# Down projections of a two-layer decoder trunk: both halves of the activation in one 512-column matmul

## The chip, the core and the metric

The kernel runs on one core of one Trainium2 chip. Five engines work side by side and meet through semaphores: TensorE (PE; its weight loads are shown as PEld), VectorE (DVE), ScalarE (ACT), GpSimd (POOL) and SyncE (SP), which issues the large DMAs. TensorE writes its sums to PSUM, eight banks of 512 float32 columns on 128 partitions; everything else lies in SBUF. The metric is the device time of one execution in microseconds (us). The kernel before takes 921.43 us, the median of three runs (919.47 to 921.58).

## The reference

The reference is a two-layer decoder trunk over 256 tokens of width 1024, in float32. Each layer has a mixer (layer 0: softmax attention beside Mamba-2 heads; layer 1: gated DeltaNet), then a gated feed-forward network, then a gated embedding of the layer. The change is inside the feed-forward network, which both layers have:

```python
D_MODEL = 1024
SEQ = 256
D_FF = 2816

def conv_ffn(h, w_gate, w_up, conv_w, conv_b, w_down):
    gte = causal_dwconv(h @ w_gate, conv_w) + conv_b.astype(h.dtype)
    return (jax.nn.silu(gte) * (h @ w_up)) @ w_down

...
        h = rmsnorm(x, norm_ffn[i])
        x = x + conv_ffn(h, ffn_w_gate[i], ffn_w_up[i], ffn_conv_w[i], ffn_conv_b[i], ffn_w_down[i])
        x = x + per_layer_embedding(x, p[i], norm_ple[i], ple_w_proj[i], ple_w_gate[i])
```

The down projection is the last product, `... @ w_down`: 2816 input features to 1024 output features for 256 tokens.

## The kernel before, in words

Activations lie transposed: features on the 128 partitions, the 256 tokens along the free dimension (`T = 256`). A matrix of 1024 features is eight tiles of 128x256, one of 2816 features is 22 tiles (`NF`).

TensorE takes float32r operands in one pass, with less precision than float32. To keep the precision, the kernel splits each operand in a high half and a low half, and `mm3` adds three products per tile of 128 input features: high weight by high activation (L188), high weight by low activation (L189), low weight by high activation (L190). Each is a matmul with 128x128 weights and 256 moving columns, and each has its own weight load, so the high weights are loaded twice.

Weights arrive in pieces of up to 1024 columns. `piece` (L140) issues the DMA from the packed stream on SP, ScalarE rounds it to the high half `whi` (L163), and VectorE, in some places GpSimd, takes the rest as the low half `wlo` (L164). Raw pieces and both halves have four buffers each, and the two split instructions are issued at a raised priority (`AHEAD = 80`), so they stand in their engines' queues well before the matmuls that use them. The order on each engine is set by the tile scheduler from those priorities; there is no table of orders. The name `lead` in `piece` shifts where a piece starts inside its buffer; it is used at two of the 22 steps of the gate and up projections alone.

Activations that TensorE streams come from `moving` (L105): one tile in which halves lie one behind the other, 256 columns each, and which starts 48 elements after an aligned address. High half and low half of one feature tile are neighbours there.

`ffn` (L277) runs in three steps. First, 22 times, gate and up tiles are made, convolved, gated and split into `ys`. Then, for each of the eight output tiles `m`, 22 feature tiles are added up in a PSUM bank `pd`, in three pieces of 8, 7 and 7 feature tiles (L310 to L314). VectorE multiplies the sum by the norm factor `Rf` on the way out (L316), adds it to the residual `x[m]` (L317), and `norm_tile` starts the next norm: ScalarE and VectorE split `x[m]` times a gain to `xp`, ScalarE squares it to `nsq`, GpSimd adds the squares up to `nss`. Last, `ple_proj` projects the layer's embedding (`pp`, 48 matmuls), `norm_end` sums the squares over partitions (`nps`, one-column matmuls at L255 and L256) and computes the norm factor, and `ple` makes the gate (`pgt`). The seven PSUM banks of the tag `acc` go round among `pg`, `pu`, `pd`, `pp` and `pgt`. So there are two stretches of down projection, one in each layer, with 8 x 22 x 3 = 528 matmuls each.

Elsewhere in the kernel, the value projection of layer 0 (L607 to L609) already has matmuls with 512 moving columns: there the weights move and the activation stands.

Of the kernel before, what the change touches and what calls it, by code (L numbers as in the profile page):

```python
# [11 lines left out]
AF = mybir.ActivationFunctionType  # L12
ALU = mybir.AluOpType
# [9 lines left out]
T = 256  # L23
# [28 lines left out]
class Trunk:  # L52
    def __init__(self, ctx, tc, stream, xT, pT, pv, tok, cst, out):
        self.tc, self.nc, self.ctx = tc, tc.nc, ctx
        self.stream, self.out = stream, out
        self.off = 0
        self.order = []
        self.n = 0
        self.pshare, self.share = 0.0, 0.0
        nc = self.nc  # L60
        ep = ctx.enter_context
        self.cpool = ep(tc.tile_pool(name="cpool", bufs=1))
        self.rawp = ep(tc.tile_pool(name="rawp", bufs=4))
        self.splp = ep(tc.tile_pool(name="splp", bufs=4))
        self.smallp = ep(tc.tile_pool(name="smallp", bufs=3))
        self.chain = ""
        self.nrm = ep(tc.tile_pool(name="nrm", bufs=1, space=PSUM))

        self.xx = self.moving(self.cpool, 2 * KD, "xx")
        warm = self.cpool.tile([P, 1], F32, tag="warm", name="warm")  # L70
        nc.vector.memset(warm, 0.0)
        nc.scalar.activation(warm, warm, AF.Exp)

        zt = self.cpool.tile([P, 256], F16, tag="zt", name="zt")
        nc.vector.memset(zt, 0.0)
        pz = self.nrm.tile([P, 512], F32, tag="nrm", name="pwarm")
        for _ in range(WARM):
            nc.tensor.matmul(pz[:, :T], zt[:, :P], zt, start=True, stop=True)
        self.pv = self.cpool.tile([P, NPV], F32, tag="pv", name="pv")
        nc.scalar.dma_start(self.pv, pv)  # L80
        xs = self.cpool.tile([P, KD, T], F32, tag="x", name="x")
        for m in range(0, KD, 2):
            nc.sync.dma_start(xs[:, m:m + 2], xT[:, m:m + 2])
        self.x = [xs[:, m] for m in range(KD)]
        self.tok = self.cpool.tile([P, 64], F32, tag="tok", name="tok")
        self.cst = self.cpool.tile([P, NCC], F32, tag="cst", name="cst")
        self.cst_src, self.tok_src = cst, tok
        self.pT = pT
        self.ones = self.cpool.tile([P, 1], F32, tag="ones", name="ones")
        nc.gpsimd.memset(self.ones, 1.0)  # L90
        self.ident = self.c("ident")
        self.id16 = self.cpool.tile([P, P], F16, tag="id16", name="id16")
        self.zb = [[self.cpool.tile([P, 4, P], F16, tag=f"zb{s}_{l}", name=f"zb{s}_{l}") for l in range(6)]
                   for s in range(1)]
# [10 lines left out]
    def moving(self, pool, n, tag):  # L105

        t = pool.tile([P, 48 + n * T], F32R, tag=tag, name=self.uid(tag), bufs=1, align_bytes=256)
        return [t[:, 48 + i * T:48 + (i + 1) * T] for i in range(n)]

    def uid(self, s):  # L110
        self.n += 1
# [69 lines left out]
    def mm3(self, out, w, a, start=True, stop=True):  # L181

        nc = self.nc
        n = len(a)
        for k in range(n):
            wh, wl = w[0][:, k], w[1][:, k]
            ah, al = a[k]
            nc.tensor.matmul(out, wh, ah, start=start and k == 0, stop=False)  # L188
            nc.tensor.matmul(out, wh, al, start=False, stop=False)  # L189
            nc.tensor.matmul(out, wl, ah, start=False, stop=stop and k == n - 1)  # L190

    def rsqrt(self, src, n, dst=None):
        nc = self.nc
        s = self.small(n, "ri", I32)
        y = self.small(n, "ry")
        nc.vector.tensor_scalar(out=s, in0=src.bitcast(I32), scalar1=1, scalar2=None,
                                op0=ALU.logical_shift_right)
        nc.vector.tensor_scalar(out=y.bitcast(I32), in0=s, scalar1=-1, scalar2=0x5F3759DF,
                                op0=ALU.mult, op1=ALU.add)
        for it in range(3):  # L200
            t = self.small(n, "rt")
            t2 = self.small(n, "rt")
            o = dst if (it == 2 and dst is not None) else self.small(n, "ry")
            nc.vector.scalar_tensor_tensor(out=t, in0=y, scalar=-0.5, in1=y, op0=ALU.mult, op1=ALU.mult)
            nc.vector.tensor_tensor(t2, t, src, op=ALU.mult)
            nc.vector.scalar_tensor_tensor(out=o, in0=t2, scalar=1.5, in1=y, op0=ALU.add, op1=ALU.mult)
            y = o
        return y
# [68 lines left out]
    def ffn(self, i, nxt):  # L277
        nc, tc = self.nc, self.tc
        with self.psum(acc=7), tc.tile_pool(name=f"ffn{i}", bufs=3) as fp:
            ys = []  # L280
            yy = self.moving(fp, 2 * NF, "yy")
            for f in range(NF):
                pg, pu = self.acc("pg"), self.acc("pu")
                both = ((pg, "ffn_w_gate"), (pu, "ffn_w_up"))

                ws = self.piece([(n, i, 0, KD, f * P, P) for _, n in both],
                                lead={KICK: (0, 16), KICK + 1: (32, 48)}.get(f, (0, 0)))
                for (ps, _), w in zip(both, ws):
                    self.mm3(ps[:, :T], w, self.a)
                g = fp.tile([P, T], F32, tag="g", name=self.uid("g"))  # L290
                nc.vector.tensor_tensor(g, pg[:, :T], self.R, op=ALU.mult)
                cw = lambda t: self.v(f"fcw{i}", f * 3 + t)
                h = fp.tile([P, T], F32, tag="h", name=self.uid("h"))
                nc.scalar.activation(h, g, AF.Identity, scale=cw(2), bias=self.v(f"fcb{i}", f))
                for s in (1, 2):
                    nc.vector.scalar_tensor_tensor(out=h[:, s:], in0=g[:, :T - s], scalar=cw(2 - s), in1=h[:, s:],
                                                   op0=ALU.mult, op1=ALU.add)
                sl = fp.tile([P, T], F32, tag="sl", name=self.uid("sl"))
                si = nc.scalar.activation(sl, h, AF.Silu)
                if i == 0 and f < len(self.zb[0]):  # L300
                    with tc.issue_after(si.ins):
                        nc.scalar.activation(self.zb[0][f], self.ident.unsqueeze(1).to_broadcast([P, 4, P]), AF.Copy)
                y = fp.tile([P, T], F32, tag="y", name=self.uid("y"))
                nc.vector.tensor_tensor(y, sl, pu[:, :T], op=ALU.mult)
                yh, yl = yy[2 * f:2 * f + 2]
                self.split(y, yh, yl)
                ys.append((yh, yl))
            self.norm_begin(f"ple{i}", fp)
            Rf = self.R
            for m in range(KD):  # L310
                pd = self.acc("pd")
                for k0, nk in ((0, 8), (8, 7), (15, 7)):
                    wd, = self.piece([("ffn_w_down", i, k0, nk, m * P, P)])
                    self.mm3(pd[:, :T], wd, ys[k0:k0 + nk], start=k0 == 0, stop=k0 == 15)  # L314
                d = fp.tile([P, T], F32, tag="pleg", name=self.uid("d"), bufs=4)
                nc.vector.tensor_tensor(d, pd[:, :T], Rf, op=ALU.mult)  # L316
                nc.vector.tensor_tensor(self.x[m], self.x[m], d, op=ALU.add)  # L317
                self.norm_tile(m)
            self.ple_proj(i, fp)
            self.norm_end()  # L320
            self.ple(i, nxt, fp)
# [831 lines left out]
```

## Time and profile before

| what | value |
|---|---|
| runs | 919.47, 921.43, 921.58 us |
| the profiled execution's own time | 923.28 us |
| its span, first to last instruction | 921.5 us |
| TensorE clock granted, mean over the span | 0.992 of full |
| PE busy | 98% of the span, 7834 matmuls |
| PEld busy | 93%, 7834 weight loads |
| DVE busy | 81% |
| ACT busy | 63% |
| down projection, layer 0 | 313.44 to 373.28 us |
| down projection, layer 1 | 827.20 to 887.04 us |

The profile is of one execution. A matmul's duration in it (276 ns for 256 columns) is longer than its share of TensorE's time, because matmuls are pipelined: the next begins before the one ahead has ended. What one costs is read from the distance between two starts. TensorE has two clock levels, 1.2 and 2.4 GHz; the granted clock is shown as 0.50 or 1.00.

### The profile page before, as it was taken

Reading aid. Unit: us, or ns where it says so; the run is one execution under the profiler, and the core shown is the slowest. Engines: PE = TensorE matmul, PEld = TensorE weight load, DVE = VectorE, ACT = ScalarE, POOL = GpSimd, SP = SyncE. Lnnn points to the kernel's source line nnn. Section 1 sums busy time; section 2 is a strip of 40 time slices with the busy share of each in tenths; the row PEclk is TensorE's granted clock in tenths of the full one; section 3 lists DMA queues with packets and bytes.
Section 4 is the critical chain, followed back from the end, with each engine's and each line's share of the span. In section 5 each row is a group of like instructions: output and inputs, shape, how many; then the busy total and the mean of one; then the engine's idle time right before and its main releaser. Section 6 shows DMA issues by size and latency. Waiting matters only on the chain. (4 is left out here: it accounts for less than half of the span.)

```text
span 921.5 us, 19977 instructions
## 1 busy us (share of the span) xinstructions
PE 900.1 (98%) x7834; PEld 860.1 (93%) x7834; DVE 747.3 (81%) x1662; ACT 584.8 (63%) x1237; POOL 42.9 (5%) x53
## 2 busy tenths in 40 slices
PE   8999999999999999999989999999999999999997
PEld 6988778999999999989889999999999999999997
DVE  6977778988888767789979998999868888876665
ACT  6577555667565545667678778787755665554552
POOL 0000112110000001010000000000002000000100
PEclk9999999999999999999989999999999999999999
DMA  7534332466666566545413333432345666666571
GB/s 276 181 122 131 93 114 92 140 197 193 203 186 197 177 203 209 169 138 158 141 47 93 114 100 108 119 113 88 122 134 177 184 194 199 190 193 189 179 227 48
DMA packets 40990, 141.40 MB, mean 153 GB/s; under 512 B 4672, under 2 KB 6208, under 8 KB 40896
## 3 DMA queue, kind: packets, MB, share of 16 engines
q1 hardware_dynamic: 40608, 139.84, 48.6%
q8 instruction: 61, 1.00, 0.4%
q10 hardware_dynamic: 288, 0.29, 0.1%
q14 instruction: 33, 0.27, 0.1%
HBM read 139.06 MB, written 1.05 MB: 152 GB/s over the span
## 5 line engine op out<-in xcount | busy, mean ns | idle before, releaser
L163 ACT ACTIVATE whi<-raw 128x1024 fp32r<-128x1024 f32 (+2 forms) x266 | 277.7, 1044 | 176.8 <-PE pd L189 38.6
L164 DVE TENSOR_TENSOR wlo<-raw,whi 128x1024 fp32r<-128x1024 f32 (+2 forms) x266 | 319.8, 1202 | 81.8 <-ACT whi L163 79.7
L188 PE MATMUL pg<-xx,whi 128*128 128x256 f32 x352 | 97.4, 277 | 0.6 <-DVE x L703 0.3
L188 PE MATMUL pu<-xx,whi 128*128 128x256 f32 x352 | 97.5, 277 | 0.0
L189 PE MATMUL pg<-xx,whi 128*128 128x256 f32 x352 | 97.4, 277 | 0.0
L189 PE MATMUL pu<-xx,whi 128*128 128x256 f32 x352 | 97.4, 277 | 0.0
L190 PE MATMUL pu<-xx,wlo 128*128 128x256 f32 x352 | 97.4, 277 | 0.0
L190 PE MATMUL pg<-xx,wlo 128*128 128x256 f32 x352 | 97.2, 276 | 0.0
L188 PE MATMUL pd<-yy,whi 128*128 128x256 f32 x352 | 97.2, 276 | 0.0
L189 PE MATMUL pd<-yy,whi 128*128 128x256 f32 x352 | 97.2, 276 | 0.0
L190 PE MATMUL pd<-yy,wlo 128*128 128x256 f32 x352 | 97.2, 276 | 0.0
L188 PE MATMUL pgd<-xx,whi 128*128 128x256 f32 x256 | 76.1, 297 | 0.4 <-DVE z L989 0.4
L190 PE MATMUL pgd<-xx,wlo 128*128 128x256 f32 x256 | 75.0, 293 | 0.0
L189 PE MATMUL pgd<-xx,whi 128*128 128x256 f32 x256 | 74.8, 292 | 0.0
L188 PEld LDWEIGHTS pg<-xx,whi 128*128 128x128 f32 x352 | 66.1, 188 | 0.8 <-issue 0.8
L188 PEld LDWEIGHTS pu<-xx,whi 128*128 128x128 f32 x352 | 66.1, 188 | 0.0
L189 PEld LDWEIGHTS pu<-xx,whi 128*128 128x128 f32 x352 | 66.1, 188 | 0.0
L190 PEld LDWEIGHTS pu<-xx,wlo 128*128 128x128 f32 x352 | 66.1, 188 | 0.0
L189 PEld LDWEIGHTS pg<-xx,whi 128*128 128x128 f32 x352 | 66.1, 188 | 0.0
L190 PEld LDWEIGHTS pg<-xx,wlo 128*128 128x128 f32 x352 | 66.1, 188 | 0.0
L188 PEld LDWEIGHTS pd<-yy,whi 128*128 128x128 f32 x352 | 66.1, 188 | 0.0
L189 PEld LDWEIGHTS pd<-yy,whi 128*128 128x128 f32 x352 | 66.1, 188 | 0.0
(357 smaller groups left out, 2636.1 us busy)
## 6 DMA issues: line engine op xcount, KB each, us to landing
raw<-stream SPq DMA_DIRECT2D x232, 512.0 KB, 3.6
raw<-stream SPq DMA_DIRECT2D x32, 448.0 KB, 3.3
x<-xT SPq DMA_DIRECT2D x4, 256.0 KB, 4.9
out<-x SPq DMA_DIRECT2D x8, 128.0 KB, 1.9
cst<-cst SPq DMA_DIRECT2D x1, 645.0 KB, 7.1
raw<-pT SPq DMA_DIRECT2D x2, 256.0 KB, 2.5
pv<-pv ACTq DMA_DIRECT2D x1, 215.5 KB, 4.4
raw<-stream SPq DMA_DIRECT2D x1, 128.0 KB, 2.0
```

Of the source, the lines that this page charges most:

```text
L163: nc.scalar.activation(hi, raw[:, :cols], AF.Copy)
L164: self.lo_engine(lo).tensor_tensor(lo_, raw[:, :cols], hi.bitcast(F32), op=ALU.subtract)
L188: nc.tensor.matmul(out, wh, ah, start=start and k == 0, stop=False)
L189: nc.tensor.matmul(out, wh, al, start=False, stop=False)
L190: nc.tensor.matmul(out, wl, ah, start=False, stop=stop and k == n - 1)
```

## The change

`moving` now also keeps, for each high half, a slice of 512 columns that covers the high half and the low half behind it. A new function `mm2` replaces `mm3` in the down projections: the high weights multiply both halves in one matmul of 512 columns, which fills the whole bank `pd`, and the low weights multiply the high half with 256 columns, added to the second half of the bank. The bank then holds high by high in its first 256 columns, and the two small products in its second. On the way out ScalarE copies the second half to SBUF, VectorE adds the first half to it, multiplies by `Rf`, and adds to the residual.

```diff
         t = pool.tile([P, 48 + n * T], F32R, tag=tag, name=self.uid(tag), bufs=1, align_bytes=256)
-        return [t[:, 48 + i * T:48 + (i + 1) * T] for i in range(n)]
+        ps = [t[:, 48 + i * T:48 + (i + 1) * T] for i in range(n)]
+        self.keep += ps
+        for i in range(0, n, 2):
+            self.both[id(ps[i])] = t[:, 48 + i * T:48 + (i + 2) * T]
+        return ps
...
+    def mm2(self, ps, w, a, start=True, stop=True):
+
+        nc = self.nc
+        n = len(a)
+        for k in range(n):
+            wh, wl = w[0][:, k], w[1][:, k]
+            ah, al = a[k]
+            nc.tensor.matmul(ps, wh, self.both[id(ah)], start=start and k == 0, stop=False)
+            nc.tensor.matmul(ps[:, T:], wl, ah, start=False, stop=stop and k == n - 1)
...
-                    self.mm3(pd[:, :T], wd, ys[k0:k0 + nk], start=k0 == 0, stop=k0 == 15)
+                    self.mm2(pd, wd, ys[k0:k0 + nk], start=k0 == 0, stop=k0 == 15)
                 d = fp.tile([P, T], F32, tag="pleg", name=self.uid("d"), bufs=4)
-                nc.vector.tensor_tensor(d, pd[:, :T], Rf, op=ALU.mult)
+                nc.scalar.activation(d, pd[:, T:], AF.Copy)
+                nc.vector.tensor_tensor(d, d, pd[:, :T], op=ALU.add)
+                nc.vector.tensor_tensor(d, d, Rf, op=ALU.mult)
                 nc.vector.tensor_tensor(self.x[m], self.x[m], d, op=ALU.add)
```

On TensorE only the down projections differ; every other matmul keeps its place in the queue. These are TensorE's rows around the first matmul of layer 0's down projection before, from the end of the up projection (`pu`) on:

```order
L190 MATMUL pu_4130<-xx_70,wlo_4140 128x256
L188 MATMUL pu_4130<-xx_70,whi_4139 128x256
L189 MATMUL pu_4130<-xx_70,whi_4139 128x256
L190 MATMUL pu_4130<-xx_70,wlo_4140 128x256
L188 MATMUL pd_4204<-yy_2568,whi_4207 128x256
L189 MATMUL pd_4204<-yy_2568,whi_4207 128x256
L190 MATMUL pd_4204<-yy_2568,wlo_4208 128x256
```

And now:

```order
L195 MATMUL pu_4130<-xx_70,wlo_4140 128x256
L193 MATMUL pu_4130<-xx_70,whi_4139 128x256
L194 MATMUL pu_4130<-xx_70,whi_4139 128x256
L195 MATMUL pu_4130<-xx_70,wlo_4140 128x256
L204 MATMUL pd_4204<-yy_2568,whi_4207 128x512
L205 MATMUL pd_4204<-yy_2568,wlo_4208 128x256
```

Three matmuls of 256 columns have become one of 512 and one of 256; over both layers that is 1056 matmuls before and 704 now, with the same number of columns.

On ScalarE the scheduler also moves the last tile's steps. ScalarE's rows at the end of the down projection in layer 0 before, where the `whi` of 5085 is the second piece of the gate after it, `nsq_4948` the square of the last residual tile and `pp` the copies of the embedding's projection:

```order
L163 ACTIVATE whi_5079<-raw_5077 128x1024
L163 ACTIVATE whi_5085<-raw_5083 128x1024
L338 ACTIVATE pp_4978<-pp_4971 128x256
L241 ACTIVATE nsq_4948<-x 128x256
L217 ACTIVATE xp_4203<-x,pv 128x256
L338 ACTIVATE pp_4987<-pp_4980 128x256
L338 ACTIVATE pp_4996<-pp_4989 128x256
L163 ACTIVATE whi_5161<-raw_5159 128x1024
```

And now, with the same pieces under the numbers 4919, 4925 and 5001, and `d_4783` the new copy:

```order
L168 ACTIVATE whi_4919<-raw_4917 128x1024
L168 ACTIVATE whi_4925<-raw_4923 128x1024
L331 ACTIVATE d_4783<-pd_4720 128x256
L355 ACTIVATE pp_4818<-pp_4811 128x256
L355 ACTIVATE pp_4827<-pp_4820 128x256
L355 ACTIVATE pp_4836<-pp_4829 128x256
L168 ACTIVATE whi_5001<-raw_4999 128x1024
L256 ACTIVATE nsq_4788<-x 128x256
L232 ACTIVATE xp_4203<-x,pv 128x256
```

The square and the split of the last residual tile now stand behind a third copy of `pp` and behind one more weight piece. VectorE's rows at the same place before:

```order
L164 TENSOR_TENSOR wlo_4968<-raw_4965,whi_4967 128x1024
L164 TENSOR_TENSOR wlo_5080<-raw_5077,whi_5079 128x1024
L316 TENSOR_TENSOR d_4945<-pd_4860,Rrep_2555 128x256
L317 TENSOR_TENSOR x<-x,d_4945 128x256
L164 TENSOR_TENSOR wlo_5086<-raw_5083,whi_5085 128x1024
L218 SCALAR_TENSOR_TENSOR xp_4203<-x,pv,xp_4203 128x256
```

And now:

```order
L169 TENSOR_TENSOR wlo_4920<-raw_4917,whi_4919 128x1024
L169 TENSOR_TENSOR wlo_4926<-raw_4923,whi_4925 128x1024
L332 TENSOR_TENSOR d_4783<-d_4783,pd_4720 128x256
L333 TENSOR_TENSOR d_4783<-d_4783,Rrep_2555 128x256
L334 TENSOR_TENSOR x<-x,d_4783 128x256
L169 TENSOR_TENSOR wlo_5002<-raw_4999,whi_5001 128x1024
L233 SCALAR_TENSOR_TENSOR xp_4203<-x,pv,xp_4203 128x256
```

The three steps that make the last `x` now stand behind the low half of the gate's second piece (4926, before 5086), which itself waits for ScalarE.

## Rows read from the trace of the kernel before

**Rows 1.** The page: busy time and share by engine; granted clock in 40 slices.

```profile
PE 900.1 (98%) x7834; PEld 860.1 (93%) x7834; DVE 747.3 (81%) x1662; ACT 584.8 (63%) x1237; POOL 42.9 (5%) x53
...
PEclk9999999999999999999989999999999999999999
```

**Rows 2.** Both down stretches by windows: from:to, length, busy by engine, clock, DMA.

```profile
313.44:373.28 59.84, 59.84 (x531) 59.84 (x529) 40.63 (x50) 30.51 (x42) 5.95 (x6) 1.00 0.63 199
827.20:887.04 59.84, 59.84 (x531) 59.84 (x529) 40.83 (x50) 30.47 (x42) 5.98 (x6) 1.00 0.63 199
```

**Rows 3.** Timeline of PE, start and duration: first down matmul, first one after.

```profile
313.44 0.28 PE L188 MATMUL pd<-yy,whi 128*128 128x256 f32 x1
...
373.28 0.28 PE L188 MATMUL pp<-pa,whi 128*128 128x256 f32 x1
```

**Rows 4.** Timeline of PE, value projection: ten 512-column matmuls in a row, first and last.

```profile
115.77 0.39 PE L609 MATMUL pv<-wlo,xx 128*128 128x512 f32 x1
...
117.83 0.40 PE L609 MATMUL pv<-wlo,xx 128*128 128x512 f32 x1
```

**Rows 5.** Timeline of PE: 256 columns on weights of 16 columns, around a clock change.

```profile
11.69 0.41 PE L189 MATMUL pdt<-xx,whi 128*16 128x256 f32 x1
11.91 0.41 PE L190 MATMUL pdt<-xx,wlo 128*16 128x256 f32 x1
...
12.29 0.28 PE L189 MATMUL pdt<-xx,whi 128*16 128x256 f32 x1
...
13.22 0.28 PE L188 MATMUL pxbc<-xx,whi 128*128 128x256 f32 x1
```

**Rows 6.** Windows of the same place, columns as in Rows 2.

```profile
10.20:11.90 1.70, 1.70 (x9) 1.14 (x8) 1.30 (x3) 1.70 (x5) 0.00 (x0) 0.50 1.00 317
12.30:13.20 0.90, 0.90 (x10) 0.74 (x8) 0.80 (x4) 0.90 (x2) 0.00 (x0) 1.00 1.01 416
```

**Rows 7.** Timeline of PE, layer 1: one float16 matmul of 512 columns and the next.

```profile
482.57 0.38 PE L892 MATMUL pR<-nid,id 128*128 128x512 f16 x1
482.79 0.22 PE L896 MATMUL pR<-S,L 128*128 128x128 f16 x1
```

**Rows 8.** Timeline of PE, output projection of layer 1: eleven matmuls, first and last.

```profile
683.00 0.28 PE L189 MATMUL pwo<-gm,whi 128*128 128x256 f32 x1
...
684.18 0.28 PE L190 MATMUL pwo<-gm,wlo 128*128 128x256 f32 x1
```

**Rows 9.** Timeline of PE: one-column matmuls on full weights.

```profile
379.08 0.36 PE L255 MATMUL nps<-ones,nss 128*128 128x1 f32 x2
379.31 0.36 PE L256 MATMUL nps<-ones,nsq 128*128 128x1 f32 x2
379.53 0.36 PE L188 MATMUL pgt<-xp,whi 128*128 128x256 f32 x1
```

**Rows 10.** Groups by shape: ScalarE's copy out of PSUM, VectorE's product out of PSUM.

```profile
L338 ACT ACTIVATE pp<-pp 128x256 f32<-128x256 f32 x16 | 5.3, 375 | 0.4 <-PE pp L190 0.4
...
L316 DVE TENSOR_TENSOR d<-pd,Rrep 128x256 f32<-128x256 f32 x16 | 6.8, 424 | 5.3 <-PE pd L190 5.2
```

**Rows 11.** Timeline of ACT, DVE and PE at the end of layer 0's down projection.

```profile
373.41 1.07 ACT L163 ACTIVATE whi<-raw 128x1024 fp32r<-128x1024 f32 x1 [1.02 <-PE pd L189]
...
374.02 0.42 DVE L317 TENSOR_TENSOR x<-x,d 128x256 f32<-128x256 f32 x1
...
374.51 1.23 DVE L164 TENSOR_TENSOR wlo<-raw,whi 128x1024 fp32r<-128x1024 f32 x1
374.64 0.41 ACT L241 ACTIVATE nsq<-x 128x256 f32<-128x256 f32 x1
...
376.13 1.07 ACT L163 ACTIVATE whi<-raw 128x1024 fp32r<-128x1024 f32 x1
...
378.72 0.28 PE L255 MATMUL nps<-ones,nss 128*128 128x1 f32 x2
```

More of the change, by code (lines that the diff above doesn't have):

```diff
@@ L57, in __init__ @@
         self.order = []
+        self.both, self.keep = {}, []
         self.n = 0
```

## The prediction

> **What bounds the kernel now.** I read the page first, then windows over the two stretches that change, then the timeline of TensorE inside them. The page shows TensorE busy for 98% of the span, at full clock in all but one of 40 slices [rows 1]. That alone does not say what a removed matmul is worth, since a busy TensorE need not be one at its peak. The windows narrow it down: in both down stretches TensorE is busy for all of the 59.84 us, at clock 1.00, while VectorE has 68% and ScalarE 51% [rows 2]. So in these stretches no other engine is late, and TensorE's own pace sets the time. That pace is read from starts, not durations: from the first down matmul at 313.44 to the first matmul after it at 373.28 there are 528 steps [rows 3], 59.84 / 528 = 0.1133 us each. The stretch in layer 1 is as long. The question is therefore only what TensorE needs per feature tile: now three steps, 0.340 us, and after the change one matmul of 512 columns and one of 256. There are 22 x 8 x 2 = 352 such pairs.
>
> **The change part by part.** The number of columns does not change: 3 x 256 before, 512 + 256 after. What goes is one matmul start and one weight load per pair. It pays only as far as those cost something now.
>
> At 2.4 GHz one column per cycle would be 256 / 2.4 = 0.1067 us, so 0.0066 us of the 0.1133 are something else. Three groups of rows bear on what. First, the value projection of layer 0 already streams 512 columns in the same number format: nine steps from 115.77 to 117.83 [rows 4], 2.06 / 9 = 0.229 us. Two steps of the down projection are 0.2267 us. A double-width matmul with half as many loads per column is not cheaper there. Second, the tiny `pdt` matmuls stream 256 columns against weights of only 16 columns. At the low clock, 0.50, a step is 0.22 us (11.69 to 11.91), which one column per cycle at 1.2 GHz would give (0.213). At the full clock eight steps from 12.29 to 13.22 take 0.93 us, 0.116 each [rows 5, 6]. So even with an eighth of the weights to load, full clock does not bring 0.107. I take from both that at full clock the float32r stream itself is a little slower than its clock, in proportion to its columns, and that the third load was hidden beside it.
>
> Price of a pair, then: the 512-column matmul between 0.2133 (the clock's floor) and 0.236 (twice the 0.118 of the slower pace in the output projection, where ten steps take 1.18 us [rows 8]); I take 0.2267, twice the present step, and not the 0.229 of the value projection, since there the roles of the two operands are exchanged and here their places in memory stay as they are. The 256-column matmul stays at 0.1133. The pair is 0.340, as before: 352 x 0 = 0 us. With 0.229 it would be 352 x 0.0023 = +0.8 us.
>
> The Trainium skill, page "TensorE: Matmul & The Clock Gate", section "Back-to-back issue gap", gives the gap between matmuls as columns over 2.4 GHz plus 2.5 ns. By that rule three matmuls would be 327.5 ns and the new pair 325 ns, and the change could save only the 2.5 ns of one start, 0.9 us in all. The rule speaks against a large gain; the trace does not agree with its size, 0.1133 against its 0.109 and 0.229 against its 0.216 [rows 3, 4].
>
> The way out costs more work on two other engines. Per output tile ScalarE gets a copy like those of `pp`, 0.375 us, and VectorE one more pass of 0.424 us [rows 10]. Over eight tiles that is 3.0 us on ScalarE (30.5 to 33.5 of 59.84) and 3.4 us on VectorE (40.6 to 44.0), still under three quarters [rows 2]; the cover is TensorE's own stream. The copy waits for TensorE's last matmul of the tile, and queued behind it on ScalarE is the next weight piece; four pieces of buffer mean that a piece is split three pieces, some 7.5 us, before it is used, against about 2.3 us for the two splits, so a copy of 0.4 us in front makes nothing late.
>
> The narrow place is the last tile, where the norm follows. Before, `x` is written from 374.02, its square from 374.64 to 375.05, and TensorE asks for the square at 378.72: 3.7 us to spare [rows 11]. Now VectorE's add stands behind the low half of the gate's second piece (374.51 to 375.74); add, product and residual at 0.42 each end at 377.0. ScalarE's square stands behind a weight piece that starts at 376.13 and ends at 377.2 [rows 11], so it ends at about 377.6. That is still 1.1 us ahead of TensorE. The cost is zero; without the 5.4 us of `pp` matmuls as cover, all 2.6 us of the delay would show, in each layer.
>
> The sum is 0 us on TensorE's path and 0 us at the ends. The profiled execution took 923.28 us for a span of 921.5, and would take the same; against the median of the runs, 921.43, I predict 921.4 us. One per mille or two may go either way in the stages after layer 0's down projection, where 0.113 and 0.118 both occur and a shifted start may choose the other.
>
> **The rivals.** The first: the 0.0066 us is paid per matmul, not per column. Then 512 columns cost 0.2133 + 0.0066 = 0.220, the pair 0.3333, and the change saves 352 x 0.0067 = 2.4 us: 919.1. For it speaks a float16 matmul of 512 columns, 482.57 to 482.79, 0.22 us [rows 7]. Against it, the value projection's 0.229 in the format at hand.
>
> The second: the weight load paces the present stream. Matmuls of a single column on full float32 weights follow each other at 0.45 / 4 = 0.1125 us (379.08 to 379.53, two in each of two rows [rows 9]), so close to 0.1133 that the stream could be waiting for loads. Then a pair with two loads costs 0.2133 for the wide matmul and 0.112 for the narrow one, 0.3253: 352 x 0.0147 = 5.2 us less, 916.2. Against it are the 16-column weights, whose step of 0.116 has no such load in it [rows 5].
>
> The third ends on the other side: the present stream is in step and the new one falls out of step. Float32r matmuls of the same shape run at 0.118 in the output projection of layer 1 [rows 8] and at 0.1133 in all 528 steps here, so there are two paces. Widths that alternate may miss the quicker. Then the narrow matmul costs 0.118 and the wide one 0.229 to 0.236, the pair 0.347 to 0.354: 2.5 to 4.9 us more, in the middle 925.1. It decides from 0.008 us per pair on. Against it, the present stream holds its mean over all 528 steps, through 24 changes of weight buffer [rows 3].
>
> The fourth: the end of the tile loop shows, since the spare time falls to 1.1 us and one more weight piece of 1.07 us in front would use it up: 0 to 2.6 us per layer, 924.0 with half of it in each.
>
> **How the numbers follow.** What a measurement of this kernel can tell from no change is about 0.3%, 2.8 us. Forecast, the pair costs what the three did: 0.53. First rival 0.16, most of it within 0.3% of before; second rival 0.12; third 0.14; fourth 0.05. Faster by over 0.3%: 0.12 from the second, 0.06 from the first, 0.03 from stages that settle otherwise, 0.21. Slower: 0.10 from the third, 0.02 from the fourth, 0.03 from such stages, 0.15. Within: 0.64. The range reaches from the second rival to the third, 916.4 to 925.0; the forecast's own range, with the 0.8 us and the stages after, is 919.9 to 923.
>
> **What would show it.** In the changed profile, the distance from the first `pd` matmul to the first `pp`: 59.8 us means the forecast, 58.7 the first rival, 57.2 the second, 61 to 62.3 the third. Starts inside a pair should lie 0.227 and 0.113 apart. TensorE should have 704 `pd` matmuls and no idle time before `nps`; idle there would be the fourth rival. The prediction is wrong in its main step if the wide matmul lies under 0.222 or over 0.234.

## The result: slower by half a per cent

The changed kernel takes 926.38 us (median of 4 runs, 924.28 to 927.17) against 921.12 us for the kernel before on the same chips: a ratio of 1.0053, 95% interval 1.004 to 1.0066. It is slower, clear of the 0.3% that a measurement can tell, and above the predicted range, 916.4 to 925.0.

The windows over the two down stretches of the changed kernel answer to [rows 2]. Columns: from:to, length, then busy time (and instructions) of PE, PEld, DVE, ACT and POOL, granted clock, DMA share, GB/s.

```profile
313.17:375.35 62.18, 62.18 (x355) 53.99 (x353) 42.59 (x57) 32.40 (x49) 5.48 (x6) 1.00 0.61 193
828.34:890.51 62.17, 62.17 (x354) 54.02 (x353) 42.66 (x57) 32.20 (x49) 5.60 (x6) 1.00 0.62 193
```

TensorE is still busy all the time at full clock, weight loads are fewer, VectorE and ScalarE are busy 2 us more (3.4 and 3.0 were forecast), and the stretch is longer: 62.18 us against 59.84, and 62.17. That is 4.7 us over both, about the 4.9 us of the ratio. (The profiled executions alone differ by less, 926.27 against 923.28 us. Outside the two stretches the changed one is 1.7 us shorter, 924.5 - 124.4 against 921.5 - 119.7; the output projection of layer 1, at 0.118 us a step in [rows 8], happens to run at 0.113 there, six steps in 0.68 us from 684.73 to 685.41.)

The timeline of TensorE shows how it begins, answering to [rows 3]. Columns: start, duration, engine, line, operation, out<-in, shapes.

```profile
313.06 0.28 PE L195 MATMUL pu<-xx,wlo 128*128 128x256 f32 x1
313.17 0.39 PE L204 MATMUL pd<-yy,whi 128*128 128x512 f32 x1
313.39 0.28 PE L205 MATMUL pd<-yy,wlo 128*128 128x256 f32 x1
313.51 0.40 PE L204 MATMUL pd<-yy,whi 128*128 128x512 f32 x1
313.75 0.28 PE L205 MATMUL pd<-yy,wlo 128*128 128x256 f32 x1
313.87 0.40 PE L204 MATMUL pd<-yy,whi 128*128 128x512 f32 x1
314.10 0.28 PE L205 MATMUL pd<-yy,wlo 128*128 128x256 f32 x1
```

Read the distances between starts. The first wide matmul takes 0.22 us, which is two of the old steps, as forecast. From the second on a wide one takes 0.235 and a narrow one 0.118: 62.18 / 176 = 0.3533 us per pair, to the end of the stretch, in both layers. TensorE leaves the stretch at the slower pace too: the 48 matmuls of `pp`, which the change does not touch, take 5.65 us now (375.35 to 381.00), 0.1177 each, against 5.44 us, 0.1133 each, before (373.28 to 378.72 [rows 3, 11]).

The end of layer 0's stretch, on VectorE, ScalarE and TensorE, answers to [rows 11]:

```profile
378.62 0.42 DVE L334 TENSOR_TENSOR x<-x,d 128x256 f32<-128x256 f32 x1
```

```profile
379.27 0.40 ACT L256 ACTIVATE nsq<-x 128x256 f32<-128x256 f32 x1
```

```profile
381.00 0.28 PE L270 MATMUL nps<-ones,nss 128*128 128x1 f32 x2
```

The square is done at 379.67, TensorE asks for it at 381.00: 1.3 us to spare, and TensorE goes from `pp` to `nps` without a gap. The longer way out is hidden. (The 0.2 us over the forecast 1.1 come from the slower `pp`: the square ends 4.3 us after the first `pp`, as forecast.)

### The profile page after: what moved, and what is told of

Read it like the earlier page. It is cut to its first block, busy times and chain, and to the rows that moved or that the text cites. A ratio compares the mean times of both kernels' runs of the same rounds, so it can differ in the third digit from the quotient of the medians.

```text
span 924.5 us, 19303 instructions
## 1 busy us (share of the span) xinstructions
PE 902.3 (98%) x7482; PEld 846.6 (92%) x7482; DVE 751.2 (81%) x1678; ACT 588.5 (64%) x1253; POOL 42.3 (5%) x53
## 5 line engine op out<-in xcount | busy, mean ns | idle before, releaser
L204 PE MATMUL pd<-yy,whi 128*128 128x512 f32 x352 | 124.4, 397 | 0.0
L204 PEld LDWEIGHTS pd<-yy,whi 128*128 128x128 f32 x352 | 66.2, 188 | 16.3
L205 PEld LDWEIGHTS pd<-yy,wlo 128*128 128x128 f32 x352 | 66.1, 188 | 0.0
L393 DVE SCALAR_TENSOR_TENSOR chh<-cg,pv,chh 128x255 f32<-128x255 f32 x132 | 63.3, 479 | 1.5 <-ACT chh L389 1.0
```

The lines of the kernel that those rows point to most:

```text
L204: nc.tensor.matmul(ps, wh, self.both[id(ah)], start=start and k == 0, stop=False)
L205: nc.tensor.matmul(ps[:, T:], wl, ah, start=False, stop=stop and k == n - 1)
```

## The experiments

Pairs and steps below are mean values, from a stretch's length over its 176 feature tiles or from rows shown. The first four kernels (up to the shift by 16 elements) have 4 to 10 runs each, against 921.40 us for the kernel before on the same chip. The shift by 48, the two kernels with 16 weight columns and the order of two and two have one run each (before: 921.57), and so have the shift by 32 and the first runs with two-byte halves (before: 919.53); of single runs the length of the stretch is used, not the time.

**Three narrow matmuls, new way out kept.** In `mm2`:

```diff
-            nc.tensor.matmul(ps, wh, self.both[id(ah)], start=start and k == 0, stop=False)
+            nc.tensor.matmul(ps[:, :T], wh, ah, start=start and k == 0, stop=False)
+            nc.tensor.matmul(ps[:, T:], wh, al, start=False, stop=False)
             nc.tensor.matmul(ps[:, T:], wl, ah, start=False, stop=stop and k == n - 1)
```

> The new way out and both halves of the bank stay, but the wide matmul is two of 256 columns again, each with its own weights, so a triple of equal matmuls. Out-of-step theory (the width breaks the quick pace): steps of 0.1133 us, down stretch 59.8 us, 921 us, same as before. Way-out theory (the extra copy and add, or the use of the second half of the bank, cost the time): stretch stays near 62.2 us and the time near 926 us.

Measured: 920.78 us, ratio 0.9994 (0.9984 to 1.0003). Its windows:

```profile
313.20:373.04 59.84, 59.84 (x530) 59.84 (x529) 42.54 (x57) 32.49 (x49) 5.23 (x6) 1.00 0.64 199
826.30:886.14 59.84, 59.84 (x530) 59.84 (x529) 42.48 (x57) 32.40 (x49) 5.42 (x6) 1.00 0.63 198
```

The stretch is as long as before to the hundredth, with the added work of ScalarE and VectorE in it. The way out and the second half of the bank cost nothing; all of the loss in the stretch comes with the wide matmul.

**All matmuls wide.**

```diff
-            nc.tensor.matmul(ps[:, T:], wl, ah, start=False, stop=stop and k == n - 1)
+            nc.tensor.matmul(ps, wl, self.both[id(ah)], start=False, stop=stop and k == n - 1)
```

> The low weights multiply both halves too, so all down matmuls have 512 columns (the sum gains a product that the kernel before leaves out). Alternation theory (widths that alternate fall out of step, equal widths keep it): 0.2267 us per wide matmul, stretch 79.8 us, about 961 us. Wide theory (a matmul of 512 columns is slow whatever its neighbour): 0.235 us each, stretch 82.7 us, about 967 us.

Measured: 965.88 us, ratio 1.0478 (1.0461 to 1.0495). Its timeline in the middle of the stretch, and the window over it:

```profile
330.08 0.39 PE L204 MATMUL pd<-yy,whi 128*128 128x512 f32 x1
330.31 0.40 PE L205 MATMUL pd<-yy,wlo 128*128 128x512 f32 x1
330.55 0.39 PE L204 MATMUL pd<-yy,whi 128*128 128x512 f32 x1
330.78 0.40 PE L205 MATMUL pd<-yy,wlo 128*128 128x512 f32 x1
331.01 0.39 PE L204 MATMUL pd<-yy,whi 128*128 128x512 f32 x1
```

```profile
312.82:394.95 82.13, 82.13 (x355) 66.18 (x353) 41.26 (x57) 32.30 (x49) 7.43 (x6) 1.00 0.47 148
```

82.13 / 352 = 0.2333 us, near the wide theory's 0.235, and the stretch is 2.3 us over the alternation theory's 79.8. Equal widths do not keep the quick pace, so alternation is not the cause; the wide matmul is.

**Wide ones first, then narrow ones, piece by piece.**

```diff
             nc.tensor.matmul(ps, wh, self.both[id(ah)], start=start and k == 0, stop=False)
+        for k in range(n):
+            wl, ah = w[1][:, k], a[k][0]
             nc.tensor.matmul(ps[:, T:], wl, ah, start=False, stop=stop and k == n - 1)
```

> Within a piece all wide matmuls come first, then all narrow ones, 8 or 7 of each in a row. Alternation theory: runs of wide ones at 0.2267 us and of narrow ones at 0.1133 us, stretch about 60 us, 921 us. Wide theory: wide ones at 0.235 us and narrow ones at 0.1133 us, stretch 61.3 us, about 924 us. If the pace of the narrow ones too stays at 0.118 us, the stretch is 62.2 us as in the changed kernel.

Measured: 923.85 us, ratio 1.0019 (1.0008 to 1.003); the stretch 61.54 us. Its timeline, where equal neighbours are merged (the last row goes on beyond the window):

```profile
311.79 2.02 PE L204 MATMUL pd<-yy,whi 128*128 128x512 f32 x8
313.66 1.07 PE L207 MATMUL pd<-yy,wlo 128*128 128x256 f32 x8
314.57 1.79 PE L204 MATMUL pd<-yy,whi 128*128 128x512 f32 x7
316.19 0.99 PE L207 MATMUL pd<-yy,wlo 128*128 128x256 f32 x7
317.02 1.80 PE L204 MATMUL pd<-yy,whi 128*128 128x512 f32 x7
318.65 0.99 PE L207 MATMUL pd<-yy,wlo 128*128 128x256 f32 x7
319.48 2.03 PE L204 MATMUL pd<-yy,whi 128*128 128x512 f32 x8
321.35 1.07 PE L207 MATMUL pd<-yy,wlo 128*128 128x256 f32 x8
322.26 0.62 PE L204 MATMUL pd<-yy,whi 128*128 128x512 f32 x2
```

Wide runs take 1.87 / 8 = 0.234 and 1.62 / 7 = 0.231 us each. The narrow runs differ: after eight wide ones 0.91 / 8 = 0.114, after seven 0.83 / 7 = 0.119. No theory had this. It suggested that a wide matmul throws the stream from one of two phases to the other, and that an even number of them brings it back. The next pieces limit that: the third comes in slow, has seven wide ones and goes out slow again (318.65 to 319.48), and the fourth comes in slow, has eight and goes out quick (321.35 to 322.26). So what decides is whether the run of wide matmuls just ahead is even or odd, and not the pace that the stream came in with, as it would be if each wide one simply switched it.

**The weights moved by 16 elements.**

```diff
-                    wd, = self.piece([("ffn_w_down", i, k0, nk, m * P, P)])
+                    wd, = self.piece([("ffn_w_down", i, k0, nk, m * P, P)], lead=(16, 16))
```

> The changed kernel with every down weight piece 16 elements (64 bytes) further on in its buffer, moving operands where they were. Address theory (the pace depends on where weights and moving operand lie to each other): the pair moves away from 0.3533 us, to 0.340 us or less, or further up. Alternation and wide theory alone: 0.3533 us and 926 us as before the shift.

Measured: 924.98 us, ratio 1.0041 (1.0029 to 1.0053); the stretch 61.79 us, a pair 0.3511 against 0.3533. The address has a part, 2 ns per pair, and not the main one. With 48 elements (`lead=(48, 48)`):

> The changed kernel with the down weights 48 elements further on in their buffers, so that they lie at the same distance from an aligned address as the moving operand. Address theory: the pace moves again, and if weights and moving operand get in each other's way at equal offsets, the pair is slower than the 0.351 us of the shift by 16 and the 0.353 us without one. If only a shift against alignment mattered, it would be like the shift by 16.

Measured: 924.39 us in one run, stretch 62.20 us, pair 0.3534: not like the shift by 16, and no worse than no shift; equal offsets are nothing special. With 32 elements (`lead=(32, 32)`):

> The changed kernel with the down weights 32 elements further on in their buffers, the last of the four offsets in steps of 16. Address theory: the pair moves again, between the 0.350 and 0.354 us seen so far or out of that band; a pair of 0.340 us or less would make the wide form worth keeping. Theory that no offset brings the wide matmul under two narrow ones: pair above 0.340 us.

Measured: 924.53 us in one run, stretch 62.18 us, pair 0.3533. None of the four offsets brings the pair near 0.340. After the shifts by 32 and 48, though, the 48 `pp` take 5.46 and 5.45 us (374.25 to 379.71, 374.44 to 379.89), the quick pace, against 5.65 without a shift.

For narrow matmuls the place of the weights does set the pace, and the kernel before already uses it. In steps 2 and 3, counted from 0, of the gate and up projections its `piece` shifts the weights by 16 (`pu`), then 32 (`pg`) and 48 (`pu`) elements. The same steps of the changed kernel in layer 0, 24 matmuls from row to row:

```profile
201.03 0.28 PE L193 MATMUL pu<-xx,whi 128*128 128x256 f32 x1
203.85 0.28 PE L193 MATMUL pg<-xx,whi 128*128 128x256 f32 x1
206.69 0.28 PE L193 MATMUL pu<-xx,whi 128*128 128x256 f32 x1
209.53 0.28 PE L193 MATMUL pg<-xx,whi 128*128 128x256 f32 x1
212.36 0.28 PE L193 MATMUL pu<-xx,whi 128*128 128x256 f32 x1
215.25 0.28 PE L193 MATMUL pg<-xx,whi 128*128 128x256 f32 x1
217.97 0.28 PE L193 MATMUL pu<-xx,whi 128*128 128x256 f32 x1
220.69 0.28 PE L193 MATMUL pg<-xx,whi 128*128 128x256 f32 x1
```

Unshifted, the stream comes in at 2.82 / 24 = 0.118 us a step; the three shifted stretches take 0.118, 0.118 and 0.120; unshifted again, it runs at 2.72 / 24 = 0.113. In the trace of the kernel before it comes in at 0.113 and goes through the same 0.118 to 0.120 (206.96 to 215.51) back to 0.113. It leaves these steps at 0.113 in both layers of every kernel traced here, and from there it runs unbroken into the down projection. That these shifts are what makes the down stretch of before quick fits all traces; a kernel without them was not run.

**Only 16 weight columns, narrow.** The first and the last tile of a sum stay whole.

```diff
+            c = P if (start and k == 0) or (stop and k == n - 1) else 16
-            nc.tensor.matmul(ps, wh, self.both[id(ah)], start=start and k == 0, stop=False)
-            nc.tensor.matmul(ps[:, T:], wl, ah, start=False, stop=stop and k == n - 1)
+            nc.tensor.matmul(ps[:c, :T], wh[:, :c], ah, start=start and k == 0, stop=False)
+            nc.tensor.matmul(ps[:c, T:], wh[:, :c], al, start=False, stop=False)
+            nc.tensor.matmul(ps[:c, T:], wl[:, :c], ah, start=False, stop=stop and k == n - 1)
```

> Three matmuls of 256 columns per feature tile as before, but all but the first and last tile of each sum use only 16 of the 128 weight columns, so the weight load is an eighth; the other 112 output features are left out. Load theory (the surplus over 0.1067 us comes from the weight load, beside or ahead of the stream): steps fall to about 0.109 us. Stream theory (the surplus belongs to the float32r stream itself): steps stay between 0.113 and 0.118 us, as the small dt projection showed 0.116.

```profile
313.29:373.13 59.84, 59.84 (x530) 50.56 (x529) 42.67 (x57) 32.35 (x49) 5.19 (x6) 1.00 0.65 200
```

An eighth of the weights, and the stretch is 59.84 us to the hundredth (the run: 920.58 us). The load has no part in the 0.1133.

**Only 16 weight columns, wide.** The same cut on the changed kernel's two matmuls.

> The changed kernel with the same cut to 16 weight columns (112 output features left out but for the first and last tile of each sum). Load theory: the wide matmul falls from 0.235 to about 0.216 us and the pair to about 0.325 us. Stream theory: the wide matmul stays at 0.226 to 0.236 us and the pair at 0.340 to 0.353 us.

```profile
312.93:374.40 61.47, 61.47 (x355) 35.08 (x353) 42.66 (x57) 32.30 (x49) 5.43 (x6) 1.00 0.63 196
```

A pair takes 61.47 / 176 = 0.3493 us, 4 ns less than with full weights, inside the stream theory's band and far from the load theory's 0.325. The run took 924.27 us. The load matters at most a little beside a wide matmul; with 16 weight columns only 16 of 128 output rows are written too, so the 4 ns need not be the load's.

**Two wide, then their two narrow ones.** In place of the loop of `mm2`:

```diff
+        for k0 in range(0, n, 2):
+            ks = range(k0, min(k0 + 2, n))
+            for k in ks:
+                nc.tensor.matmul(ps, w[0][:, k], self.both[id(a[k][0])], start=start and k == 0, stop=False)
+            for k in ks:
+                nc.tensor.matmul(ps[:, T:], w[1][:, k], a[k][0], start=False, stop=stop and k == n - 1)
```

> The changed kernel with two wide matmuls, then their two narrow ones, all products kept. Phase theory (each wide matmul shifts the stream by half a beat, so that an even number of them brings the narrow ones back in step, an odd number leaves them out): 0.226, 0.236, 0.118, 0.114 us, that is 0.694 for two tiles, 0.347 per tile, stretch near 61.1 us plus a little for the odd tile of the two pieces of 7. Without such a phase the steps would be those of the changed kernel, 0.235 and 0.118, stretch 62.2 us.

```profile
313.31 0.62 PE L204 MATMUL pd<-yy,whi 128*128 128x512 f32 x2
313.78 0.39 PE L206 MATMUL pd<-yy,wlo 128*128 128x256 f32 x2
314.01 0.62 PE L204 MATMUL pd<-yy,whi 128*128 128x512 f32 x2
314.47 0.39 PE L206 MATMUL pd<-yy,wlo 128*128 128x256 f32 x2
314.70 0.62 PE L204 MATMUL pd<-yy,whi 128*128 128x512 f32 x2
```

Four matmuls take 0.46 + 0.23 = 0.69 us, and (314.70 - 313.31) / 4 = 0.3475 per feature tile, as the phase theory said; the stretch is 61.12 us, the run 923.41 us. So the same matmuls with the same operands cost 1.06 us less per stretch by order alone. That the pace hangs on the order is shown, and even the best order tried loses to three narrow matmuls.

**Two-byte halves, wide.** Weights and activations of the down projections are split into bfloat16 halves. The edit without the lines that hand the number format through `moving` and `piece`:

```diff
-                    wd, = self.piece([("ffn_w_down", i, k0, nk, m * P, P)])
+                    wd, = self.piece([("ffn_w_down", i, k0, nk, m * P, P)], dt=BF16)
...
-            yy = self.moving(fp, 2 * NF, "yy")
+            yy = self.moving(fp, 2 * NF, "yy", BF16)
...
-                self.split(y, yh, yl)
+                nc.scalar.activation(yh, y, AF.Copy)
+                nc.vector.tensor_tensor(yl, y, yh, op=ALU.subtract)
```

> The changed kernel with both operands of the down projections in bfloat16 halves instead of float32r halves (the splits keep fewer bits, so the down projection is less precise). Theory that the surplus belongs to the four-byte stream: wide matmul about 0.216 us, narrow about 0.109 us, pair 0.325 us, stretch 57.2 us, some 5 us less than before. Theory that any matmul of 512 columns loses the beat: wide 0.226 to 0.236 us as with float32r.

One run gave 916.33 us. The same with three narrow matmuls:

> The same bfloat16 halves in three matmuls of 256 columns. Four-byte theory: 0.109 us each, 0.327 us per feature tile, stretch 57.5 us, so that width saves only one start, 0.002 us per tile. If a 256-column step is bound by something else than the stream's bytes, it stays at 0.113 us and the stretch at 59.8 us.

One run gave 916.87 us. Then five runs of each on one chip, against 920.99 us for the kernel before:

> The wide form with bfloat16 halves, timed. From its pace (0.325 us per pair against 0.340 before) 352 x 0.015 = 5.3 us less than before on TensorE, less what the first look already gave back outside the stretch (ends of the stretches at 114.6 to 116.9 instead of 119.7 us in sum): 916 us, faster than before by 0.3 to 0.6%. If the one look was a lucky run, within 0.3% of before.

> Three narrow matmuls with bfloat16 halves, timed on the same chip. Four-byte theory: 0.327 us per tile, 0.7 us more than the wide form over both layers, not to be told from it: 916 to 917 us, faster than before. If the wide form were worth more than a start once the beat is not at stake, this kernel would be over 2.8 us slower than the wide one.

Measured: wide 915.25 us, ratio 0.9936 (0.9923 to 0.995); narrow 916.46 us, ratio 0.9948 (0.9935 to 0.996). Both are faster than before; their intervals overlap, so the wide form's 1.2 us over the narrow one isn't settled by the times. The windows, wide kernel first:

```profile
312.48:369.61 57.13, 57.13 (x355) 34.38 (x353) 42.40 (x57) 32.60 (x49) 4.67 (x6) 1.00 0.68 206
822.86:879.99 57.13, 57.13 (x354) 34.39 (x353) 42.47 (x57) 32.54 (x49) 4.88 (x6) 1.00 0.68 206
```

```profile
312.75:370.32 57.57, 57.57 (x530) 51.61 (x529) 42.36 (x57) 32.58 (x49) 4.71 (x6) 1.00 0.68 205
822.53:880.10 57.57, 57.57 (x530) 51.61 (x529) 42.45 (x57) 32.52 (x49) 4.94 (x6) 1.00 0.67 204
```

A pair takes 57.13 / 176 = 0.3246 us, three narrow ones 57.57 / 176 = 0.3271. So in two bytes the wide form does save one start, 2.5 ns per tile, 0.9 us in all, and the surplus over 0.1067 falls from 6.6 to 2.4 ns per step: 57.57 / 528 = 0.1090. Most of the surplus, and the loss of the wide form, belong to the float32r format. Whether it is the four bytes of the stream as such stays open: the halves also lie at other distances in bytes, and the load, which shrinks too, is set aside only as far as the kernels with 16 weight columns go.

## Why the prediction was wrong

**What bounds the kernel**: right. TensorE's pace alone sets the two stretches; every experiment moved their length by its steps, with no other engine late.

**The price of a pair**: this step failed. "The 512-column matmul [...] I take 0.2267, twice the present step, and not the 0.229 of the value projection" held for one matmul, the first; the others took 0.235, and the narrow one beside it 0.118 instead of 0.1133. 352 x (0.3533 - 0.340) = 4.7 us is the loss in the two stretches; the slower `pp` behind them adds 0.2 each. The mistake was to take the quick pace as a property of the columns. It is a state of the stream: 528 narrow float32r matmuls with their weights at one place kept it, one wide matmul ended it. The trace of before had warned: 0.118 in [rows 8], a mean of 0.229 over the nine steps of [rows 4], which I put down to the exchanged operands, and the narrow steps that slow down where the weights are shifted.

**The surplus belongs to the stream, not to the load**: right for narrow matmuls, by the 16-column kernel, which keeps 0.1133. The second rival, the load that paces the stream, falls with it; the first, a surplus paid per matmul, falls with the wide matmuls, which it puts at a pair of 0.3333: no order with float32r came under 0.347.

**The third rival** is what happened, at the upper end of its price, 0.354 us, 4.9 us more, and its sign, a stretch of 61 to 62.3 us, is the one that was seen. It had a chance of 0.14, and the range stopped at its middle. The reason against it, that the present stream holds its mean over 528 steps, was no evidence: all of them were narrow, with weights at one place. Its mechanism was right in that the stream falls out of step, and wrong in that widths that alternate do it: equal wide ones run at 0.2333.

**The way out** and **the end of the tile loop**: right. The kernel with the new way out and narrow matmuls takes 0.9994 of before, and the spare time at the last tile is 1.3 us against 1.1 forecast. The fourth rival falls.

**The rule of the page** "TensorE: Matmul & The Clock Gate" of the Trainium skill, section "Back-to-back issue gap", columns over 2.4 GHz plus 2.5 ns: the bfloat16 kernels agree with it (0.109 per narrow step, 0.325 per pair), and with it the 0.9 us that it allowed the change. The float32r traces do not: 0.113 to 0.120 for 256 columns and, on average, 0.231 to 0.235 for 512 in the rows shown.

Open: what in the chip sets the two phases. Counted run by run, the traces without a shift agree: after an even run of wide matmuls (eight, two) the narrow ones get back to 0.113, after an odd one (seven, or the single wide matmul of each pair in the changed kernel) they stay at 0.118. That is why the changed kernel never gets back. Why an even run should do it is not shown, and with the weights shifted by 32 or 48 elements the rule fails: single wide matmuls leave the `pp` behind them quick.

## What to carry to other kernels

Count matmul time by the distance of starts, and before merging narrow matmuls into wide ones look for a trace of the wide form in the same number format: if it has one, its price is a better estimate than a sum of narrow ones. Here it would have been better, not good: 0.229 gives 0.8 of the 4.7 us, because the wide ones took 0.235 and their narrow neighbours slowed down too. So a short trace of the very mixture is worth more than either. In float32r a removed weight load was worth nothing where the stream already covered it, and a 512-column matmul with its 256-column neighbour cost more than three of 256 in each order tried here. Where the precision allows two-byte halves, they gained more here, 0.5 to 0.6% of this kernel, and only then did the wide form save its one start.

## What the runs showed of the hardware

TensorE at its granted full clock ran float32r matmuls of 256 columns at two steady paces, 0.1133 and 0.118 us, and in these stretches it kept the one it had settled on while the weights' place did not change: 528 steps in a row at the first in the kernel before, the 48 of `pp` at the second right after the changed stretch. With weights shifted by 16 to 48 elements narrow steps of the gate and up projections took 0.118 to 0.120 us, and after the shifted steps the stream was quick, whichever pace it had before. The number of weight columns, 16 or 128, does not change the quick pace. At the low clock the surplus does not appear: eight steps from the row below to 11.91 [rows 5] take 1.71 us, 0.214 each, against 0.2133 for one column per cycle. In bfloat16 2.4 ns of its 6.6 are left.

```profile
10.20 0.41 PE L188 MATMUL pdt<-xx,whi 128*16 128x256 f32 x1
```
